# A hybrid decoder trunk on one core: the SSD branch product by seven half-size products, and gate multiplications on GpSimd

## Chip, core and metric

The kernel runs on one core of a Trainium2 chip. The metric is the time of one execution on the device, in microseconds (us). TensorE is called PE, its weight loads PEld, VectorE DVE, ScalarE ACT, GpSimd POOL; SP is the engine whose queue issues the DMA transfers.

## The reference

One layer of a decoder trunk with 1024 tokens and width 1024. The input is normalised and projected; three token mixers run side by side on the projection: attention in a window (branch A), gated linear attention, GLA (B), and a Mamba-2 state-space scan, SSD (C). Each mixer gives 512 channels, which a SiLU gate multiplies; each is projected to 1024 channels by its own matrix; sigmoid gates of the layer's input merge the three; an output projection and a residual add follow.

```python
y_a = sliding_window_attention(q, k, v, attn_sinks) * jax.nn.silu(ag)
y_b = rms_norm(o_b, gla_out_norm).reshape(b, s, GLA_VALUE_WIDTH) * jax.nn.silu(gg)
y_c = gated_group_rms_norm(y_c.reshape(b, s, SSD_D_INNER), sz, ssd_out_norm, SSD_GROUPS)
branches = jnp.stack([y_a, y_b, y_c], axis=2)
u = jnp.einsum("bsnw,nwd->bsnd", branches, w_branch)
gates = jax.nn.sigmoid(mg.reshape(b, s, N_BRANCH, D_MODEL))
merged = jnp.sum(gates * u, axis=2)
return x + merged @ w_out
```

## The kernel before

Activations lie with channels on partitions: a block of 128 channels by 512 tokens is one tile, and 1024 tokens are two halves. Every product keeps float32 precision by three matmuls: an operand is split into a rounded part (hi, an ACT cast to a 32-bit matmul format) and the remainder (lo, a subtraction), and hi·hi, hi·lo and lo·hi are added up in one PSUM bank.

Large projections by pairs of 128 output channels (`dense_pair`, called by `pair_fm`) use a seven-product form: the operand h is there in seven blocks or sums of blocks (11, 21, 22, t1, t2, t3, t4n), and seven products p1 to p7 take the place of eight. Weight sums and some remainders are made on POOL (lines 332 and 265). Such a pair is gg, which gives the gates of branch B: `branch_gates` (line 1050) takes its rows, loads the mixer's output (tile ggy, line 1056), forms the SiLU by a tanh on ACT and a multiplication on DVE (line 1058), multiplies (line 1059) and stores (line 1060) to ybg_d. It is called twice, for channels 0 and 2.

Then come the branch products. `load_y` loads a branch's 512 gated channels in eight blocks through three buffers (tags t1, t2, tx of the pool sums), casts each on ACT (line 1078) and makes its remainder on DVE (line 1079). `gated(n, d, y)` computes output block d (a unit) of branch n: it loads 128x512 weights, casts them on ACT, makes the remainder on DVE or POOL (line 265), loads the merge gate tg, and for each half runs 12 matmuls (line 1104) and one DVE multiplication by the gate (line 1107). The loop over d runs branch C (n = 2, tiles u2 in the order of instructions) two units ahead of branch A (n = 0); the sum of both goes to t_d (lines 1119, 1120). Then `merged` does branch B (n = 1), adds t_d, and `part` and `diff` make the seven sums for the output products (`dense_pair` on w_o).

The order of the instructions on each engine is set by a scheduler when the program is built: each engine, and SP's queue of transfers, then takes its own in that order and waits at the first that isn't ready. Buffers come from pools: big (14 tiles, held by h's seven sums until gg is done), big2 (4), sums (3), w2 (10 tiles of 128x512 for weights, sums and ggy), st (4 of 128x1024: gates and products), and PSUM in two pools of 4 banks.

Of the kernel before, what the change touches and what calls it, by code (L numbers as in the profile page):

```python
# [81 lines left out]
def kernel(  # L82
# [173 lines left out]
    def work(dt, name):  # L256
        return wpool.tile([P, 512], dt, tag="w2", bufs=NW2, name=name)
# [243 lines left out]
    for k in range(4):  # L501
# [10 lines left out]
                    in1=rowv[:, R_IF : R_IF + 32].unsqueeze(1).to_broadcast([P, NT, 32]), op=ALU.mult)  # L512
# [7 lines left out]
    first = True  # L520
    for a, i in ((a2, 3), (a1, 4), (a2, 2), (a1, 3), (a2, 1), (a1, 2), (a2, 0), (a1, 1), (a1, 0)):
# [8 lines left out]
        first = False  # L530
# [66 lines left out]
    with tc.tile_pool(name="att", bufs=2) as mp, tc.tile_pool(name="att1", bufs=1) as mp1:  # L597
# [63 lines left out]
        for t in range(NT):  # L661
            nk = P if t == 0 else 2 * P
            mk = amask[:, P * (1 - t % 2) : P * (1 - t % 2) + nk]
            nm = mp.tile([P, 8], F32, tag="nm", name=f"nm{t}")
# [34 lines left out]
            for g in range(2):  # L699
# [448 lines left out]
    for k in range(4):  # L1148
        b11, b12 = merged(k)
# [67 lines left out]
```

## Time and profile before

| | us |
|---|---|
| median of 3 runs (lowest, highest) | 998.47 (997.79, 998.58) |
| the profiled execution, its own time | 995.85 |
| its span, first to last instruction | 994.1 |
| PE busy in it | 944.2 |
| DVE busy | 765.0 |
| POOL busy | 491.2 |
| ACT busy | 451.1 |

Busy time of a group is the number of its instructions by their mean. A matmul's own duration (about 390 ns) overlaps with the next one's; what one adds to a row of them is the distance of their starts. "Idle before" is the time an engine stood still ahead of an instruction, with what ended it. Times in a timeline or a window count from the span's start.

### The profile page before, as it was taken

To read this page: it belongs to the slowest core of one execution; us is meant where nothing else is said; L and a number is where in the kernel's file an instruction comes from. 1 tells how busy PE (TensorE), PEld (TensorE's weight loads), DVE (VectorE), ACT (ScalarE), POOL (GpSimd) and SP (SyncE) were. 2 spreads that over 40 slices of the span, in tenths; PEclk is the share of its full clock that TensorE was granted. 3 is DMA by queue.
4 is the path that set the end of the run, shared out by engine and by line. 5 is a ranking of instruction groups with operands and counts; after the bars stand their busy time and mean duration, and the time that the engine had idled before them with its cause. 6 is when DMAs were issued, how large, how long until landed. Compare 5 with 4: busy or idle time off the path is not lost.

```text
span 994.1 us, 14844 instructions
## 1 busy us (share of the span) xinstructions
PE 944.2 (95%) x5089; PEld 795.8 (80%) x5089; DVE 765.0 (77%) x1228; ACT 451.1 (45%) x1014; POOL 491.2 (49%) x442
## 2 busy tenths in 40 slices
PE   8989888999999998999989999999999999997998
PEld 7989788988868777778778887878887878875786
DVE  6899787877998988876887858667868754599644
ACT  6442344366566556556545555344444411133221
POOL 5754556854562662344455644454533001256776
PEclk9999889999999999999999999999999999999999
DMA  9402142423232332241595635365465876763443
GB/s 365 180 27 85 54 160 67 142 88 111 78 119 85 107 97 99 77 136 42 193 297 190 210 129 157 120 201 180 128 209 199 280 239 217 239 207 103 163 146 116
DMA packets 84410, 150.14 MB, mean 151 GB/s; under 512 B 7328, under 2 KB 40304, under 8 KB 84336
## 3 DMA queue, kind: packets, MB, share of 16 engines
q1 hardware_dynamic: 84160, 149.18, 45.0%
q8 instruction: 40, 0.66, 0.3%
q14 instruction: 34, 0.28, 0.1%
q10 hardware_dynamic: 176, 0.02, 0.0%
HBM read 101.96 MB, written 47.22 MB: 150 GB/s over the span
## 4 chain that ended last, share of the span: by engine, by line
PE 40%; DVE 12%; DMA 8%; issue 7%; POOL 5%; ACT 5%; SPq 0%; POOLq 0%; DVEq 0%; ACTq 0%
PE ps_p_mg L320 14%; PE ps_p_o L320 5%; PE ps_p_ag L320 4%; PE ps_u L1104 3%; PE ps_p_cv L320 3%; DMA tg<-tg_d 2%; PE ps_p_gqk L320 2%; DVE acc L749 1%; DMA tl<-t_d 1%; DMA yc_r<-yc_d 1%; PE py L928 1%; PE ppv L715 1%; DMA yb_r<-ybg_d 1%; POOL s_o L332 1%; PE psc L677 1%
## 5 line engine op out<-in xcount | busy, mean ns | idle before, releaser
L320 PE MATMUL ps_p_mg<-ht_hi,wh_p_mg 128*128 128x512 f32 x192 | 75.9, 395 | 0.0
L320 PE MATMUL ps_p_mg<-ht_lo,wh_p_mg 128*128 128x512 f32 x192 | 75.7, 394 | 0.0
L320 PE MATMUL ps_p_mg<-ht_hi,wl_p_mg 128*128 128x512 f32 x192 | 75.7, 395 | 0.0
L340 DVE TENSOR_TENSOR c_mg<-ps_p_mg,c_mg 128x512 f32<-128x512 f32 x84 | 56.3, 681 | 12.6 <-PE ps_p_mg L320 8.1
L265 POOL TENSOR_TENSOR wl_p_mg<-s_mg,wh_p_mg 128x512 fp32r<-128x512 f32 x24 | 33.7, 1404 | 54.0 <-ACT wh_p_mg L262 46.3
L265 POOL TENSOR_TENSOR wl_u<-wr_u,wh_u 128x512 fp32r<-128x512 f32 x8 | 10.6, 1331 | 98.6 <-ACT wh_u L262 98.5
L320 PE MATMUL ps_p_mg<-h_hi,wl_p_mg 128*128 128x512 f32 x144 | 57.1, 396 | 0.0
L320 PE MATMUL ps_p_mg<-h_lo,wh_p_mg 128*128 128x512 f32 x144 | 56.6, 393 | 0.0
L320 PE MATMUL ps_p_mg<-h_hi,wh_p_mg 128*128 128x512 f32 x144 | 56.5, 392 | 0.0
L1107 DVE SCALAR_TENSOR_TENSOR tg<-tg,ps_u 128x512 f32<-128x512 f32 x48 | 31.9, 682 | 27.1 <-DMA tg<-tg_d 26.2
L262 ACT CAST wh_p_mg<-s_mg 128x512 fp32r<-128x512 f32 x48 | 29.6, 617 | 49.0 <-POOL s_mg L332 31.0
L265 DVE TENSOR_TENSOR wl_p_mg<-wr_mg,wh_p_mg 128x512 fp32r<-128x512 f32 x36 | 38.4, 1074 | 15.7 <-ACT wh_p_mg L262 8.9
L749 DVE SCALAR_TENSOR_TENSOR acc<-c_cv,cwh,acc 128x512 f32<-128x512 f32 (+3 forms) x48 | 41.8, 888 | 4.7 <-ACT acc L746 4.6
L320 PEld LDWEIGHTS ps_p_mg<-ht_hi,wh_p_mg 128*128 128x128 f32 x192 | 36.1, 188 | 7.2
L320 PEld LDWEIGHTS ps_p_mg<-ht_hi,wl_p_mg 128*128 128x128 f32 x192 | 36.1, 188 | 7.2
L320 PEld LDWEIGHTS ps_p_mg<-ht_lo,wh_p_mg 128*128 128x128 f32 x192 | 36.1, 188 | 7.1
L342 DVE SCALAR_TENSOR_TENSOR c_o<-ps_p_o,c_o 128x512 f32<-128x512 f32 x28 | 18.9, 688 | 26.5 <-POOL c_o L346 16.7
L690 ACT ACTIVATE sc<-sc,nm 128x256 f32<-128x256 f32 (+1 forms) x64 | 30.9, 485 | 18.1 <-DVE nm L685 18.1
L262 ACT CAST wh_u<-wr_u 128x512 fp32r<-128x512 f32 x24 | 14.7, 620 | 47.1 <-PE ps_u L1104 43.8
L733 ACT ACTIVATE c_mg<-c_mg 128x1024 f32<-128x1024 f32 x24 | 25.4, 1056 | 15.3 <-DVE c_mg L340 12.5
L320 PEld LDWEIGHTS ps_p_mg<-h_lo,wh_p_mg 128*128 128x128 f32 x144 | 27.1, 188 | 5.4
L320 PEld LDWEIGHTS ps_p_mg<-h_hi,wl_p_mg 128*128 128x128 f32 x144 | 27.1, 188 | 5.3
(479 smaller groups left out, 3456.8 us busy)
## 6 DMA issues: line engine op xcount, KB each, us to landing
wr_mg<-in_w_fm_dram SPq DMA_DIRECT2D x24, 512.0 KB, 4.0
tg_d<-c_mg SPq DMA_DIRECT2D x24, 512.0 KB, 2.6
tg<-tg_d SPq DMA_DIRECT2D x24, 512.0 KB, 4.3
wr_u<-in_w_br_dram SPq DMA_DIRECT2D x24, 256.0 KB, 3.9
xq<-in_xf_dram SPq DMA_DIRECT2D x8, 512.0 KB, 10.7
wr_cv<-in_w_fm_dram SPq DMA_DIRECT2D x8, 512.0 KB, 3.5
xbc_d<-acc SPq DMA_DIRECT2D x16, 256.0 KB, 2.6
e<-acs_dram SPq DMA_DIRECT2D x16, 256.0 KB, 5.4
```

The costliest lines, as they stand in the source:

```text
L262: A.copy(hi[:, :n], raw)
L265: (lo_eng or V).tensor_tensor(out=lo[:, :n], in0=raw, in1=hi[:, :n].bitcast(F32), op=ALU.subtract)
L320: T.matmul(ps, lhsT=l[:, k, :], rhs=r, start=n == 0, stop=n == 3 * kt - 1)
L332: G.tensor_tensor(out=o, in0=a, in1=b, op=op)
L340: V.tensor_tensor(out=o, in0=p, in1=c, op=op)
L342: V.scalar_tensor_tensor(out=o, in0=p, scalar=scale, in1=c, op0=ALU.mult, op1=op)
L677: T.matmul(psc[:, 256 * j : 256 * j + nk], lhsT=qT[:, h, :], rhs=kT[:, g, l, :nk], start=l == 0, stop=l == 1)
L690: A.activation(out=sc[:, j, :nk], in_=sc[:, j, :nk], func=AF.Exp, bias=nm[:, h : h + 1], accum_out=dn[:, h : h + 1])
L733: A.activation(out=c, in_=c, func=AF.Tanh, scale=0.5)
L749: V.scalar_tensor_tensor(out=acc[:, z:], in0=r[:, o + z - d : o + 512 - d], scalar=cwh[:, 4 * c + 3 - d : 4 * c + 4 - d], in1=acc[:, z:], ...
L1104: T.matmul(ps, lhsT=l[:, k, :], rhs=r, start=m_ == 0, stop=m_ == 11)
L1107: V.scalar_tensor_tensor(out=o, in0=o, scalar=1.0, in1=ps, op0=ALU.add, op1=ALU.mult)
```

## The change

`branch_gates` takes the engine for its last multiplication as an argument; for gg it is POOL, for branch A's gates it stays DVE. Branch C's operand is no longer four blocks per half but seven: 11, 21, 22 are blocks of its 2 x 2 division (channels by tokens), t3, t1, t2, t4n differences made on POOL; each has two parts k of 128x512 and is split by ACT and DVE as before. The blocks and t3 are made around the first gg pair (`y_blocks`), the other sums after the second (`y_sums`), for which the raw blocks are loaded again. `gated_pair` computes two units at once from weight blocks and sums of 128x256 by seven products of six matmuls, with the sums of weights on POOL, and the combinations of products on DVE and ACT in the tile cr. Remainders of the weights are made on POOL, but for the first two products. Branch A's weight remainders move from DVE to POOL too, and the loop goes by pairs.

```diff
-    def branch_gates(u0, f, y, dst, name):
+    def branch_gates(u0, f, y, dst, name, eng=V):
...
-                V.tensor_tensor(out=ys, in0=ch, in1=ys, op=ALU.mult)
+                eng.tensor_tensor(out=ys, in0=ch, in1=ys, op=ALU.mult)
...
-    y_c = load_y(big2_tile, yc_d, "yc", lambda: branch_gates(U_GG, 0, yb_d, ybg_d, "gg"))
-    branch_gates(U_GG, 2, yb_d, ybg_d, "gg")
+    def y_raw(f, hf, tag):
+        raw = sums.tile([P, 512], F32, tag=tag, name=f"yc_r{f}{hf}")
+        Q.dma_start(raw, yc_d[:, f, hf * 512 : hf * 512 + 512])
+        return raw
...
+    def y_part(key, k, a):
...
+        hi, lo = (p[:, k, :] for p in y_c[key])
+        A.copy(hi, a)
+        V.tensor_tensor(out=lo, in0=a, in1=hi.bitcast(F32), op=ALU.subtract)
+
+    def y_diff(key, k, o, a, b):
+        G.tensor_tensor(out=o, in0=a, in1=b, op=ALU.subtract)
+        y_part(key, k, o)
+
+    def y_blocks(k):
+        b12, b22 = y_raw(k, 1, "t2"), y_raw(k + 2, 1, "tx")
+        y_part("11", k, y_raw(k, 0, "t1"))
+        y_part("22", k, b22)
+        y_diff("t3", k, b12, b22, b12)
+        y_part("21", k, y_raw(k + 2, 0, "t1"))
+
+    def y_sums(k):
+        b11, b12, b22 = y_raw(k, 0, "t1"), y_raw(k, 1, "t2"), y_raw(k + 2, 1, "tx")
+        y_diff("t1", k, b11, b12, b11)
+        b21 = y_raw(k + 2, 0, "t2")
+        y_diff("t2", k, b22, b22, b11)
+        y_diff("t4n", k, b21, b21, b22)
+
+    y_blocks(0)
+    branch_gates(U_GG, 0, yb_d, ybg_d, "gg", G)
+    y_blocks(1)
+    branch_gates(U_GG, 2, yb_d, ybg_d, "gg", G)
+    for k in range(2):
+        y_sums(k)
...
+    def gated_pair(n, d):
+
+        raw = wpool.tile([P, 1024], F32, tag="wraw", name=f"wr_u{n}_{d}")
...
+        cr = big_tile(F32, f"cr{n}_{d}")
+        c11, c12, c21, c22 = (cr[:, i, :] for i in range(4))
+
+        def mul(w, key, ps, nm, first=True, last=True, eng=G):
+            wt = work(F32R, f"wp_u{n}_{d}{nm}")
+            A.copy(wt[:, :256], w)
+            eng.tensor_tensor(out=wt[:, 256:], in0=w, in1=wt[:, :256].bitcast(F32), op=ALU.subtract)
+            m_ = 0
+            for k in range(2):
...
+                for l, r in ((hi, r_hi), (hi, r_lo), (lo, r_hi)):
+                    T.matmul(ps, lhsT=l, rhs=r, start=first and m_ == 0, stop=last and m_ == 5, skip_group_check=True)
...
+        b1 = mtile(f"ps_u{n}_{d}_p1")
+        G.tensor_tensor(out=s1, in0=a21, in1=a22, op=ALU.add)
+        mul(a11, "11", b1, "p1", last=False, eng=V)
+        A.copy(c11, b1)
+        b2 = bank("p2")
+        mul(a12, "21", b2, "p2", eng=V)
+        G.tensor_tensor(out=a21, in0=a11, in1=a21, op=ALU.subtract)
+        G.tensor_tensor(out=s2, in0=s1, in1=a11, op=ALU.subtract)
+        V.tensor_tensor(out=c11, in0=b2, in1=c11, op=ALU.add)
+        gate(c11, 0, 0)
+        b7 = bank("p7")
+        mul(a21, "t3", b7, "p7")
+        mul(s2, "t2", b1, "p6", first=False, last=False)
+        A.copy(c12, b1)
+        G.tensor_tensor(out=a12, in0=a12, in1=s2, op=ALU.subtract)
+        V.tensor_tensor(out=c22, in0=b7, in1=c12, op=ALU.add)
+        b5 = bank("p5")
+        mul(s1, "t1", b5, "p5")
...
+        mul(a22, "t4n", b4, "p4")
...
+        mul(a12, "22", b1, "p3", first=False)
...
-    for d in range(KT + 2):
+    for d in range(0, KT + 2, 2):
...
-            tcs[d] = gated(2, d, y_c)
+            crs[d] = gated_pair(2, d)
...
-            tc_, ta = tcs.pop(d - 2), gated(0, d - 2, y_a)
...
+                ta = gated(0, d - 2 + i, y_a, G)
```

How the order moves, at three places. First, POOL after the last gg product's weight remainder (wl_p3_gg2; s and wl are weight sums and remainders). Before:

```order
L332 TENSOR_TENSOR s3_gg2_7943<-wr_gg2_1_7879,wr_gg2_2_7881 128x512
L265 TENSOR_TENSOR wl_p5_gg2_7982<-s1_gg2_7903,wh_p5_gg2_7981 128x512
L332 TENSOR_TENSOR s4_gg2_8000<-wr_gg2_1_7879,s2_gg2_7923 128x512
L265 TENSOR_TENSOR wl_p3_gg2_8003<-s4_gg2_8000,wh_p3_gg2_8002 128x512
L265 TENSOR_TENSOR wl_u1_0_8730<-wr_u1_0_8727,wh_u1_0_8729 128x512
```

Now (yc_r are raw blocks of branch C, numbered by channel block and half, and the sums made in their place; ggy the gate multiplications of branch B; s_u2, wr_u2 and wp_u2 weight sums and remainders of the first pair):

```order
L265 TENSOR_TENSOR wl_p3_gg2_8005<-s4_gg2_8002,wh_p3_gg2_8004 128x512
L1108 TENSOR_TENSOR yc_r20_8060<-yc_r20_8060,yc_r21_8054 128x512
L1186 TENSOR_TENSOR s_u2_0_8091<-wr_u2_0_8088 128x256
L1191 TENSOR_TENSOR wr_u2_0_8088<-wr_u2_0_8088 128x256
L1192 TENSOR_TENSOR s_u2_0_8091<-s_u2_0_8091,wr_u2_0_8088 128x256
L1059 TENSOR_TENSOR ggy200_8023<-c1_gg2_7885,ggy200_8023 128x512
L1169 TENSOR_TENSOR wp_u2_0p7_8124<-wr_u2_0_8088,wp_u2_0p7_8124 128x256
L1199 TENSOR_TENSOR wr_u2_0_8088<-wr_u2_0_8088,s_u2_0_8091 128x256
L1169 TENSOR_TENSOR wp_u2_0p6_8133<-s_u2_0_8091,wp_u2_0p6_8133 128x256
L1169 TENSOR_TENSOR wp_u2_0p5_8146<-s_u2_0_8091,wp_u2_0p5_8146 128x256
L1059 TENSOR_TENSOR ggy20512_8030<-c1_gg2_7885,ggy20512_8030 128x512
L1108 TENSOR_TENSOR yc_r10_8070<-yc_r11_8072,yc_r10_8070 128x512
```

Where POOL had nothing until branch B's weights, 20 instructions follow up to the second t4n sum: the eleven below the first row here, then one remainder, a gate multiplication, a weight sum of the second pair, a remainder, the last gate multiplication, the second t2 sum, two weight sums, and the second t4n sum.

Second, PE after the last gg product, in branch C's first two pairs (ps_u2_0 and ps_u2_2; p1 holds p1, p6 and p3 one after the other; the operand's name tells which). Before, 12 matmuls of one unit and half follow 12 of the next. Now, from the 27th matmul of branch C on:

```order
L1175 MATMUL ps_u2_2_p1_8227<-yc11_7680,wp_u2_2p1_8229 128x512 x2
L1175 MATMUL ps_u2_2_p2_8239<-yc21_7692,wp_u2_2p2_8240 128x512 x2
L1175 MATMUL ps_u2_2_p1_8227<-yc11_7680,wp_u2_2p1_8229 128x512 x4
L1175 MATMUL ps_u2_2_p2_8239<-yc21_7692,wp_u2_2p2_8240 128x512 x4
L1175 MATMUL ps_u2_0_p5_8145<-yct1_8057,wp_u2_0p5_8146 128x512
L1175 MATMUL ps_u2_0_p4_8157<-yct4n_8067,wp_u2_0p4_8158 128x512
L1175 MATMUL ps_u2_0_p5_8145<-yct1_8057,wp_u2_0p5_8146 128x512 x2
L1175 MATMUL ps_u2_0_p1_8097<-yct2_8063,wp_u2_0p6_8133 128x512
L1175 MATMUL ps_u2_2_p7_8253<-yct3_7687,wp_u2_2p7_8254 128x512 x2
L1175 MATMUL ps_u2_0_p1_8097<-yct2_8063,wp_u2_0p6_8133 128x512 x2
L1175 MATMUL ps_u2_0_p4_8157<-yct4n_8067,wp_u2_0p4_8158 128x512
L1175 MATMUL ps_u2_2_p7_8253<-yct3_7687,wp_u2_2p7_8254 128x512 x4
```

The second pair's first two products have moved in between the first pair's k = 0 and k = 1 parts; the row yct4n in the last but one place is the 48th matmul of branch C and the first that reads the second t4n block.

Third, SP's queue, from the loads of the second `y_sums` on. Before, six of the eight loads of branch A's operand (ya_r) were issued among the gg transfers. Now:

```order
L1096 DMA yc_r10_8070<-yc_d_4740 128x512
L1096 DMA yc_r31_8074<-yc_d_4740 128x512
L1096 DMA yc_r11_8072<-yc_d_4740 128x512
L1060 DMA ybg_d_2918<-ggy200_8023 128x512
L1060 DMA ybg_d_2918<-ggy20512_8030 128x512
L1161 DMA tg2_2_8222<-tg_d_2916 128x1024
L1096 DMA yc_r30_8079<-yc_d_4740 128x512
L1060 DMA ybg_d_2918<-ggy210_8037 128x512
L171 DMA wr_u0_1_8350<-in_w_br_dram 128x512
L1060 DMA ybg_d_2918<-ggy21512_8044 128x512
L1161 DMA tg2_3_8224<-tg_d_2916 128x1024
L1076 DMA ya_r00_8186<-yag_d_2917 128x512
```

All loads of branch A's operand have moved behind the last loads of branch C's and behind the stores of branch B's last gate multiplications.

## Rows read from the trace of the kernel before

**Rows 1.** Page: busy time and share of each engine; the span in 40 slices.
```profile
PE 944.2 (95%) x5089; PEld 795.8 (80%) x5089; DVE 765.0 (77%) x1228; ACT 451.1 (45%) x1014; POOL 491.2 (49%) x442
...
PEclk9999889999999999999999999999999999999999
```

**Rows 2.** Windows: busy PE, PEld, DVE, ACT, POOL; clock, DMA share, GB/s.
```profile
768.00:857.00 89.00, 87.38 (x385) 71.73 (x384) 50.85 (x73) 20.05 (x34) 5.14 (x4) 1.00 0.72 241
904.00:936.00 32.00, 26.67 (x103) 19.52 (x102) 27.11 (x30) 11.14 (x19) 25.12 (x18) 0.95 0.34 116
...
726.00:857.00 131.00, 127.25 (x559) 103.78 (x558) 84.26 (x117) 39.34 (x68) 19.96 (x14) 1.00 0.70 233
```

**Rows 3.** Chain that ended last, in order of time: start us, us, what.
```profile
813.71 32.94 PE ps_u L1104 x144
```

**Rows 4.** Timeline of PE: start us, us, line, operation, out<-in.
```profile
768.11 0.39 PE L1104 MATMUL ps_u<-yc_hi,wh_u 128*128 128x512 f32 x1
...
769.92 0.39 PE L1104 MATMUL ps_u<-yc_hi,wl_u 128*128 128x512 f32 x1
...
857.34 0.39 PE L1104 MATMUL ps_u<-yb_hi,wh_u 128*128 128x512 f32 x1
```

**Rows 5.** Waits of PE, 740 to 860: total us, times, longest.
```profile
PE ps_p_gg L320 <- ACT wh_p_gg L262: 1.9, 2, 1.1
PE ps_u L1104 <- DVE tg L1107: 1.6, 2, 1.2
```

**Rows 6.** Groups of DVE from 726 to 768: busy us, mean ns, idle before.
```profile
L340 DVE TENSOR_TENSOR c_gg<-ps_p_gg,c_gg 128x512 f32<-128x512 f32 x13 | 8.7, 683 | 1.7 <-PE ps_p_gg L320 1.6
L1079 DVE TENSOR_TENSOR yc_lo<-yc_r,yc_hi 128x512 fp32r<-128x512 f32 x8 | 7.0, 909 | 2.6 <-ACT yc_hi L1078 2.6
L265 DVE TENSOR_TENSOR wl_p_gg<-wr_gg,wh_p_gg 128x512 fp32r<-128x512 f32 x4 | 4.1, 1018 | 1.7 <-ACT wh_p_gg L262 1.7
```

**Rows 7.** Groups of the whole span by form: DVE and ACT.
```profile
L1107 DVE SCALAR_TENSOR_TENSOR tg<-tg,ps_u 128x512 f32<-128x512 f32 x48 | 31.9, 682 | 27.1 <-DMA tg<-tg_d 26.2 <-PE ps_u L1104 0.8
L645 DVE TENSOR_TENSOR qh<-qk,qh 128x256 fp32r<-128x256 f32 x24 | 13.5, 577 | 0.8 <-ACT qh L644 0.7
L644 ACT CAST qh<-qk 128x256 fp32r<-128x256 f32 x24 | 8.9, 404 | 16.1 <-DVE qk L632 16.0
```

**Rows 8.** A group of ACT from 726 to 768.
```profile
L1078 ACT CAST yc_hi<-yc_r 128x512 fp32r<-128x512 f32 x8 | 4.9, 620 | 8.6 <-DMA yc_r<-yc_d 8.6
```

**Rows 9.** Groups of POOL by form.
```profile
L629 POOL TENSOR_TENSOR t<-qk,tb 128x256 f32<-128x256 f32 x16 | 12.8, 820 | 8.5 <-issue 2.8 <-ACT c_cv L752 1.8 <-ACT es L687 1.7
L265 POOL TENSOR_TENSOR wl_p_gg<-s_gg,wh_p_gg 128x512 fp32r<-128x512 f32 x4 | 5.9, 1470 | 15.9 <-ACT wh_p_gg L262 8.4 <-DVE ggy L1059 7.5
```

**Rows 10.** Timeline of POOL: start us, us, what, idle before.
```profile
759.79 1.74 POOL L332 TENSOR_TENSOR s_gg<-wr_gg,s_gg 128x512 f32<-128x512 f32 x1
762.26 1.57 POOL L265 TENSOR_TENSOR wl_p_gg<-s_gg,wh_p_gg 128x512 fp32r<-128x512 f32 x1 [0.73 <-ACT wh_p_gg L262]
836.31 1.29 POOL L265 TENSOR_TENSOR wl_u<-wr_u,wh_u 128x512 fp32r<-128x512 f32 x1 [72.48 <-ACT wh_u L262]
```

**Rows 11.** Line 629's instructions: ns min/median/max, two forms together.
```profile
L629 POOL TENSOR_TENSOR t<-qk,tb x32: 315/740/1193, 156.9 to 369.5; 128x256 f32<-128x256 f32 x16, 128x64 f32<-128x64 f32 x16
```

**Rows 12.** Timeline of DVE behind the last gg product.
```profile
773.18 0.68 DVE L1059 TENSOR_TENSOR ggy<-c_gg,ggy 128x512 f32<-128x512 f32 x1
```

**Rows 13.** Timeline of SP's queue: issues of the operands' loads.
```profile
733.28 1.58 SPq L1076 DMA_DIRECT2D yc_r<-yc_d  x3
...
764.99 1.76 SPq L1076 DMA_DIRECT2D ya_r<-yag_d  x2
```

**Rows 14.** Loads of yc_r, then of ya_r: us from issue to landing.
```profile
DMA to landing us min/median/max: 3.0/4.1/5.2
...
DMA to landing us min/median/max: 2.8/5.5/7.1
```

**Rows 15.** DMA issues from 715 to 800: count, KB each, median us to landing.
```profile
tg<-tg_d SPq DMA_DIRECT2D x6, 512.0 KB, 5.7
```

More of the change, by code (lines that the diff above doesn't have):

```diff
@@ L1088 @@
     merge_gates(1, U_MGB, 6)
-    y_c = load_y(big2_tile, yc_d, "yc", lambda: branch_gates(U_GG, 0, yb_d, ybg_d, "gg"))
-    branch_gates(U_GG, 2, yb_d, ybg_d, "gg")
+    y_c = {}
+    def y_raw(f, hf, tag):
[3 more added lines that the diff above has]
+    def y_part(key, k, a):
+        if k == 0:
+            t = (big_tile if key in ("t1", "t2", "t4n") else big2_tile)(F32R, f"yc{key}")
+            y_c[key] = (t[:, 0:2], t[:, 2:4])
+        hi, lo = (p[:, k, :] for p in y_c[key])
[22 more added lines that the diff above has]
+        y_sums(k)
     def gated(n, d, y, lo_eng=None):
@@ L1108, in gated, with bank, gate @@
         return tg
+    def gated_pair(n, d):
+        raw = wpool.tile([P, 1024], F32, tag="wraw", name=f"wr_u{n}_{d}")
+        for i in range(2):
+            Q.dma_start(raw[:, 512 * i : 512 * i + 512], w_br[8 * n + d + i])
+        a11, a12, a21, a22 = (raw[:, 256 * i : 256 * i + 256] for i in range(4))
+        s = work(F32, f"s_u{n}_{d}")
+        s1, s2 = s[:, :256], s[:, 256:]
+        tgs = []
+        for i in range(2):
+            tg = st_tile(f"tg{n}_{d + i}")
+            Q.dma_start(tg, tg_d[n, d + i])
+            tgs.append(tg)
+        cr = big_tile(F32, f"cr{n}_{d}")
[6 more added lines that the diff above has]
+            for k in range(2):
+                r_hi, r_lo = (p[:, k, :] for p in y_c[key])
+                hi, lo = wt[:, k * P : k * P + P], wt[:, 256 + k * P : 256 + k * P + P]
+                for l, r in ((hi, r_hi), (hi, r_lo), (lo, r_hi)):
+                    T.matmul(ps, lhsT=l, rhs=r, start=first and m_ == 0, stop=last and m_ == 5, skip_group_check=True)
+                    m_ += 1
+        def bank(nm):
+            return psd1.tile([P, 512], F32, tag="d1", name=f"ps_u{n}_{d}_{nm}")
+        def gate(c, i, hf):
+            V.scalar_tensor_tensor(out=c, in0=tgs[i][:, hf * 512 : hf * 512 + 512], scalar=1.0, in1=c, op0=ALU.add, op1=ALU.mult)
+        b1 = mtile(f"ps_u{n}_{d}_p1")
[16 more added lines that the diff above has]
+        mul(s1, "t1", b5, "p5")
+        e5 = half_tile(f"p5_u{n}_{d}")
+        A.copy(e5, b5)
+        b4 = bank("p4")
+        mul(a22, "t4n", b4, "p4")
+        V.tensor_tensor(out=c21, in0=b4, in1=c22, op=ALU.add)
+        gate(c21, 1, 0)
+        V.tensor_tensor(out=c22, in0=e5, in1=c22, op=ALU.add)
+        gate(c22, 1, 1)
+        mul(a12, "22", b1, "p3", first=False)
+        V.tensor_tensor(out=c12, in0=b1, in1=e5, op=ALU.add)
+        gate(c12, 0, 1)
+        return cr
@@ L1110 @@
     t_d = dram.tile([KT, P, S], F32, name="t_d")
-    tcs = {}
-    for d in range(KT + 2):
+    crs = {}
+    for d in range(0, KT + 2, 2):
         if d == 2:
@@ L1115 @@
         if d < KT:
-            tcs[d] = gated(2, d, y_c)
+            crs[d] = gated_pair(2, d)
         if d >= 2:
-            tc_, ta = tcs.pop(d - 2), gated(0, d - 2, y_a)
-            V.tensor_tensor(out=tc_, in0=tc_, in1=ta, op=ALU.add)
-            Q.dma_start(t_d[d - 2], tc_)
+            cr = crs.pop(d - 2)
+            for i in range(2):
+                ta = gated(0, d - 2 + i, y_a, G)
+                V.tensor_tensor(out=ta, in0=ta, in1=cr[:, 2 * i : 2 * i + 2, :].rearrange("p f l -> p (f l)"), op=ALU.add)
+                Q.dma_start(t_d[d - 2 + i], ta)
     y_b = load_y(big_tile, ybg_d, "yb")
```

## The prediction

> **What bounds the kernel now.** I read the page first: TensorE is busy 95% of the span, DVE 77%, the other two under half, and TensorE's granted clock is at its upper level, 2.4 GHz, in nearly every slice [rows 1]. Then the stages around the change [rows 2]: from 768 to 857 us, where the SSD and attention branch products run, PE has 87.4 of 89 us, DVE 50.9, ACT 20.1, POOL 5.1. So PE bounds this stage. Between 904 and 936 it has holes: 26.7 of 32. The chain of waits goes straight through the branch products: 32.94 us of nothing but matmuls [rows 3]. The timeline of PE gives the frame [rows 4]: the first SSD product starts at 768.11 (I call this moment E), the first GLA product at 857.34, so 89.2 us for 384 matmuls; eight steps from 768.11 to 769.92 are 1.81 us, 0.227 us per matmul, 87.1 us in all. Some 2.1 us of the stage is idle, 1.6 of them behind a gate multiplication of DVE; the product before E loses 1.9 us to ACT casts [rows 5].
>
> What reaches the end: a later start of the GLA products moves everything behind them, since their tail is bound by DVE work that starts with them. I take 1:1.
>
> **The change, part by part.**
>
> *Matmuls.* A pair of units has 48 matmuls now, 7 products x 2 blocks x 3 = 42 afterwards; four pairs: 24 fewer, all of the same 128x512 form. 24 x 0.227 = **-5.4 us**.
>
> *Work of DVE and ACT.* DVE loses 8 gate multiplications and 16 weight remainders of 0.68 us (-16.3), gains 20 sums of 0.68, 8 half-width remainders of 0.58 and 6 operand remainders of 0.91 (+23.7) [rows 6, 7]: +7.4 us on a DVE with 38 us free from 768 to 857 [rows 2]. ACT gains about 28 half casts at 0.40 against 8 at 0.62, 12 copies and 6 casts at 0.62: +17 on 20 of 89 us [rows 2, 7, 8]. As sums both are hidden by the free time of these engines; in order, they are not, which the DVE rival below prices.
>
> *Work of POOL.* Added: 8 gate multiplications and 8 operand sums at 1.47, 36 half-width ones at 0.82, 8 weight remainders of the attention units at 1.29: 23.5 + 29.5 + 10.3 = 63 us, on 20 busy of the 131 us from 726 to 857 [rows 2, 9, 10]. As a sum that fits too, and POOL now stands still for 72.48 us there [rows 10]. What matters is the order. In the queue of POOL after the remainder for the last gg product, 20 instructions stand up to and with the second t4n sum, which the first pair needs: 8 of 512 columns (3 operand sums k=1, one k=0, 4 gate multiplications) and 12 of 256. None may be passed.
>
> Wide price: 1.47 mean, with ends 1.29 and 1.74 [rows 9, 10]. Narrow price: 128x256 is measured elsewhere at 0.82 mean, which I take; the low end is a straight line from the shortest 64-column one (0.315) to 1.29 at 512 columns, 0.73; the high end for a mean of twelve is half of 1.74, 0.87 (one alone took up to 1.19) [rows 9 to 11]. Chain: 8 x 1.47 + 12 x 0.82 = 21.6 us (19.1 to 24.4), and an ACT cast of 0.6. In the same time PE has only 10 matmuls of the last gg product and 47 in front of the first that reads the second t4n block: 57 x 0.227 = 12.9 us. If POOL gets to the queue's head when PE does, PE stands still for 21.6 + 0.6 - 12.9 = **+9.3 us** (6.8 to 12.1).
>
> A head start lowers that. Now the last gg remainder ends at 763.83 [rows 10], 2.0 us before PE wants it (E minus 10 matmuls = 765.84). But it has a floor, because the gate multiplications need the last gg product itself: the second now starts 5.1 us after E [rows 12], no sooner than 3 us (DVE add, tanh, DVE gate, 0.7 each, and issue). From that one on, 6 wide and 5 narrow remain: 11.4 us at the low prices, so the block is there at E + 15.0, and PE asks for it at E + 47 x 0.227 = 10.7. So the stall is at least 4.3 us unless a price is lower than any row.
>
> The Trainium skill's page "SBUF — State Buffer", section "Who interferes with whom", says that a DVE instruction with two SBUF inputs and a GpSimd instruction that reads SBUF exclude each other for their whole length, which speaks against moving multiplications from one to the other. The trace agrees so far: DVE adds with one operand in PSUM keep to 0.683, remainders with both in SBUF have means of 0.909 and 1.018 in the stretch with POOL work [rows 6]. By that rule as a strict one, each POOL step would stand behind DVE's, at the high end of the chain (24.4), and the time would be 1009.7; by the mean rows it is the sum below.
>
> *Operand of SSD.* Instead of 8 loads through three buffers there are 16, and six of them pass one buffer (t1), one after the other: r00, r20, r10, r30, then r00 again for the first sum. A link is load 4.1, cast 0.62, remainder 0.91: 5.6 us [rows 6, 8, 14]. The first lands near 738.4 (third of three issues from 733.28 on, 0.5 apart) [rows 13], its remainder is done at 739.9; three links give 756.7, the reload lands at 760.8. Behind it on POOL, in order: sum t1, two instructions of gg, sum t2, and the last gg remainder, 5 x 1.47: 768.2. Ten matmuls later E is 770.4 instead of 768.1. At the shortest loads (3.0) a link is 4.3 and nothing shifts. Range 0 to 2.4, taken: **+2 us**, since the median load is nearer.
>
> *Operand of the attention branch.* Its loads use the same three buffers, so they now start after the t1, t2, t4n sums of k=1, where today six of eight are issued before 768 [rows 13]. Through t1 go r00, r03, r10 (links of 5.5 + 0.62 + 0.68 = 6.8 us) [rows 6, 8, 14]. The third hi part is there 3 x 6.8 - 0.7 = 19.7 us after the second t2 sum; PE asks for it 3.1 us (one wide and two narrow POOL steps to the t4n sum) + 0.6 (cast) + 49 x 0.227 = 14.8 us after that sum. Stall 4.9 us at the median load; none at the shortest (2.8). Taken: **+2.5 us**, the middle, since the median comes from a stretch with more transfers at a time.
>
> *The rest.* Eight loads more, 2 MB, raise the DMA share of 726 to 857 from 0.70 (233 GB/s, 30 MB) to about 0.75: hidden. A PE that waits can lose clock: between 904 and 936, with 26.7 of 32 us busy, it was granted 0.95 [rows 2]; 5% of the 26 us behind E is 1.3 us, an upper end that I leave out of the sum. Order and number of the GLA and output products stay.
>
> **Sum.** -5.4 + 2 + 9.3 + 2.5 = +8.4 us. The profiled execution took 995.85 us (span 994.1 and 1.75 around it), so it would be 1004.3; the median of the runs shown, 998.47, is 2.6 above the profiled one, and on it the sum gives **1006.9 us**. A difference under 0.2% (2 us) can't be told from none by such measurements.
>
> **Rivals.**
>
> *POOL hides everything, faster.* For it: POOL has 111 of 131 us free, and the first four products of a pair need only early blocks. Then -5.4 stands alone: 993.1, or 991 if the idle 2.1 goes too. It is decided at one place: the second t4n sum must end within 10 us of E. Against it: the gate multiplications in front of it wait for the last gg product, and the floor above gives 4.3. With the floor and no other stall, -1.1: 997.4. I give faster by over 2 us 0.18.
>
> *No change.* The stall lies between 3.4 and 7.4 in sum: floor case, or short loads with an early POOL; also if the tail's DVE work, not its start, sets the end. 998.5, chance 0.12.
>
> *DVE's queue stands at a gate load, much slower.* The first attention gate's load needs a buffer that the first pair's last gate frees, and behind its multiplication on DVE stand the second pair's sums, which hold PSUM banks that PE wants. A gate load takes 5.7 us [rows 15] and could come wholly on top: +14, 1012.6. For it: DVE already waits 26.2 us for gate loads today [rows 7]. Against: PE lost only 1.6 us to that [rows 5]. Chance 0.12.
>
> The forecast itself, slower by 2 to 12 us, has 0.58. So faster 0.18, same 0.12, slower 0.70. The range goes from 995.3 (floor -1.1 and the idle 2.1 recovered) to 1016 (12.1 + 2.4 + 4.9 - 5.4 = +14.0, and 3.5 of a gate load or of lost clock).
>
> **What would show it.** Right: PE has 24 fewer matmuls; between E and the first attention product PE idles 7 to 12 us, put down to ACT casts and POOL; POOL is over 80% busy for 25 us from E; the t4n sum of k=1 ends 16 to 20 us after E; E is at 768 to 771; the GLA products start 6 to 12 us later than 857.3. Each stage's matmuls keep 0.227 us. Wrong: half-width POOL work far under 0.73, the second t4n sum within 10 us of E, or GLA products starting before 857.

## The result, and the profile after

The changed kernel takes 1011.79 us (median of 4 runs, 1010.65 to 1013.16), the kernel before, on the same chip, 998.13 us (4 runs, 994.81 to 998.58). The ratio is 1.0135, 95% interval 1.0111 to 1.016: slower by 13.7 us. The prediction said 1006.9, between 995.3 and 1016.0.

The page of the changed kernel, busy time and clock by slices; before, in [rows 1], DVE had 765.0, POOL 491.2, and the clock was below the top digit in two slices instead of four:

```profile
PE 952.8 (94%) x5065; PEld 797.4 (79%) x5065; DVE 785.5 (78%) x1238; ACT 466.6 (46%) x1052; POOL 558.7 (55%) x502
...
PEclk9999988999999999999999999999999899998999
```

TensorE has 24 matmuls fewer (5065 against 5089) and is busy 8.6 us longer. The timeline of PE in the changed kernel gives the stages by four starts: the first gg product, the first SSD product (E), the first attention product, the first GLA product.

```profile
727.74 0.39 PE L320 MATMUL ps_p_gg<-h_hi,wh_p_gg 128*128 128x512 f32 x1
...
774.31 1.98 PE L1175 MATMUL ps_u_p<-yc,wp_u_0p 128*128 128x512 f32 x8
...
782.79 2.42 PE L1175 MATMUL ps_u_p<-yc,wp_u_2p 128*128 128x512 f32 x8 [0.25 <-ACT wp_u_2p L1168]
...
786.96 0.63 PE L1175 MATMUL ps_u_p<-yct,wp_u_0p 128*128 128x512 f32 x2
792.19 0.80 PE L1175 MATMUL ps_u_p<-yct,wp_u_0p 128*128 128x512 f32 x1 [4.60 <-ACT yct L1104]
...
804.04 0.50 PE L1144 MATMUL ps_u<-ya_hi,wh_u 128*128 128x512 f32 x1 [1.10 <-ACT p_u L1204]
...
872.42 0.39 PE L1144 MATMUL ps_u<-yb_hi,wh_u 128*128 128x512 f32 x1
```

Windows over the same four stages (columns as in [rows 2]), the kernel before:

```profile
726.54:768.11 41.57, 39.45 (x173) 31.70 (x172) 32.95 (x44) 19.11 (x33) 14.82 (x10) 1.00 0.65 217
768.11:784.43 16.32, 16.32 (x73) 13.52 (x72) 13.45 (x22) 6.97 (x12) 0.00 (x0) 1.00 0.96 340
784.43:857.34 72.91, 71.29 (x313) 58.41 (x312) 37.66 (x51) 13.11 (x23) 5.14 (x4) 1.00 0.67 218
857.34:994.10 136.76, 124.08 (x529) 99.22 (x527) 93.85 (x112) 38.12 (x64) 87.45 (x60) 0.99 0.48 160
```

and the changed kernel, where the last two rows cut out the wait of 4.60 us and what follows it:

```profile
727.74:774.31 46.57, 41.50 (x173) 32.47 (x172) 32.47 (x37) 18.91 (x33) 28.45 (x20) 0.96 0.67 217
774.31:804.04 29.73, 21.97 (x74) 14.45 (x72) 20.02 (x23) 14.16 (x31) 29.11 (x27) 0.89 0.63 196
804.04:872.42 68.38, 66.04 (x288) 54.01 (x289) 58.16 (x70) 21.47 (x43) 32.45 (x28) 1.00 0.74 244
872.42:1011.50 139.08, 126.71 (x529) 101.19 (x527) 92.81 (x110) 38.23 (x64) 86.07 (x60) 0.96 0.48 157
...
787.40:792.10 4.70, 0.19 (x1) 0.00 (x0) 0.00 (x0) 1.17 (x2) 4.70 (x6) 1.00 0.64 209
792.10:798.00 5.90, 5.30 (x12) 3.54 (x13) 4.01 (x4) 4.35 (x11) 5.90 (x7) 0.50 0.67 190
```

The two profiled spans differ by 17.4 us and the medians by 13.7: the profiled execution of the changed kernel lies 1.4 over its median, that of the kernel before 2.3 under. The 17.4 lie so: 1.2 ahead of gg, 5.0 in the gg stage, 13.4 between E and the first attention product, -4.5 up to the GLA products, 2.3 in the tail. The first is not the change's: that start lies anywhere from 723.2 to 729.5 in the profiles below. In the second window PE is busy 21.97 us for the 72 matmuls that took 16.32, and idle for 7.8: it waits, and then runs at the lower clock. Behind the 4.60 us the granted clock is 0.50, the level of 1.2 GHz, and 12 matmuls take 6.2 us (792.19 to 798.40, 0.5 of it a second wait) instead of 2.7.

POOL's timeline in the changed kernel shows what those 4.60 us waited for: the cast of the second t2 sum, which POOL makes from 790.22 on. The first row is the last gg remainder, the last the second t4n sum:

```profile
770.53 1.29 POOL L265 TENSOR_TENSOR wl_p_gg<-s_gg,wh_p_gg 128x512 fp32r<-128x512 f32 x1
771.78 1.74 POOL L1108 TENSOR_TENSOR yc_r<-yc_r,yc_r 128x512 f32<-128x512 f32 x1
...
790.22 1.26 POOL L1108 TENSOR_TENSOR yc_r<-yc_r,yc_r 128x512 f32<-128x512 f32 x1
791.44 0.72 POOL L1191 TENSOR_TENSOR wr_u<-wr_u 128x256 f32<-128x256 f32 x1
792.12 0.73 POOL L1192 TENSOR_TENSOR s_u<-s_u,wr_u 128x256 f32<-128x256 f32 x1
792.81 1.72 POOL L1108 TENSOR_TENSOR yc_r<-yc_r,yc_r 128x512 f32<-128x512 f32 x1
```

Twenty instructions without a gap of note, 771.8 to 794.5: 22.7 us.

### The profile page after: what moved, and what is told of

The parts are those of the page before. It is cut to its first block, busy times and chain, and to the rows that moved or that the text cites. A ratio compares the mean times of both kernels' runs of the same rounds, so it can differ in the third digit from the quotient of the medians.

```text
span 1011.5 us, 14965 instructions
## 1 busy us (share of the span) xinstructions
PE 952.8 (94%) x5065; PEld 797.4 (79%) x5065; DVE 785.5 (78%) x1238; ACT 466.6 (46%) x1052; POOL 558.7 (55%) x502
## 4 chain that ended last, share of the span: by engine, by line
PE 42%; DVE 15%; issue 8%; POOL 7%; DMA 7%; ACT 5%; SPq 0%; POOLq 0%; DVEq 0%; ACTq 0%
PE ps_p_mg L320 12%; PE ps_p_o L320 5%; PE ps_u L1144 4%; PE ps_p_ag L320 4%; PE ps_p_gv L403 3%; PE ps_p_cv L320 2%; DVE acc L749 2%; PE ps_p_gqk L320 2%; PE ps_u_p L1175 2%; DMA tl<-t_d 1%; DVE sc L680 1%; DVE c_mg L340 1%; DVE wl_p_mg L265 1%; ACT sc L690 1%; PE psc L677 1%
## 5 line engine op out<-in xcount | busy, mean ns | idle before, releaser
L749 DVE SCALAR_TENSOR_TENSOR acc<-c_cv,cwh,acc 128x512 f32<-128x512 f32 (+3 forms) x48 | 41.9, 889 | 4.9 <-ACT acc L746 4.8
L265 POOL TENSOR_TENSOR wl_u<-wr_u,wh_u 128x512 fp32r<-128x512 f32 x16 | 23.8, 1497 | 38.5 <-ACT wh_u L262 24.3
L320 PEld LDWEIGHTS ps_p_mg<-ht_hi,wl_p_mg 128*128 128x128 f32 x192 | 36.2, 189 | 7.8 <-DVE wl_p_mg L265 0.7
L320 PEld LDWEIGHTS ps_p_mg<-ht_lo,wh_p_mg 128*128 128x128 f32 x192 | 36.2, 189 | 7.1
L342 DVE SCALAR_TENSOR_TENSOR c_o<-ps_p_o,c_o 128x512 f32<-128x512 f32 x28 | 18.9, 688 | 27.5 <-POOL c_o L346 17.4
L320 PEld LDWEIGHTS ps_p_mg<-h_hi,wh_p_mg 128*128 128x128 f32 x144 | 27.2, 189 | 5.4
L1144 PE MATMUL ps_u<-yb_hi,wh_u 128*128 128x512 f32 x64 | 25.9, 405 | 3.0 <-DVE tg L1147 3.0
```

Of the source, the lines that this page charges most:

```text
L265: (lo_eng or V).tensor_tensor(out=lo[:, :n], in0=raw, in1=hi[:, :n].bitcast(F32), op=ALU.subtract)
L320: T.matmul(ps, lhsT=l[:, k, :], rhs=r, start=n == 0, stop=n == 3 * kt - 1)
L342: V.scalar_tensor_tensor(out=o, in0=p, scalar=scale, in1=c, op0=ALU.mult, op1=op)
L749: V.scalar_tensor_tensor(out=acc[:, z:], in0=r[:, o + z - d : o + 512 - d], scalar=cwh[:, 4 * c + 3 - d : 4 * c + 4 - d], in1=acc[:, z:], ...
```

## The experiments

Twelve kernels, each timed beside the kernel before (medians of 997.3 for e1 to e4, 997.7 for e5 to e8, 997.9 for e9 to e11, 998.3 for e12). The profiled execution of each is cut at the same four starts (us; "head" is E to the first attention product, "rest" from there to the first GLA product, "branch" both):

| | time (ratio, 95% interval) | gg | head | rest | branch | tail |
|---|---|---|---|---|---|---|
| before | | 41.6 | 16.3 | 72.9 | 89.2 | 136.8 |
| the change | 1011.8 (1.0111 to 1.016) | 46.6 | 29.7 | 68.4 | 98.1 | 139.1 |
| e1 gates on DVE | 1011.3 (1.012 to 1.0194) | 43.1 | 27.3 | 69.9 | 97.2 | 143.2 |
| e2 gates alone | 1004.0 (1.0058 to 1.0091) | 44.9 | 16.3 | 75.7 | 92.0 | 136.5 |
| e3 shorter t1 chain | 1014.3 (1.0145 to 1.0204) | 46.1 | 32.7 | 66.1 | 98.8 | 145.3 |
| e4 sums on DVE | 1015.5 (1.0161 to 1.0203) | 45.7 | 26.8 | 73.3 | 100.1 | 140.3 |
| e5 gates left out | 1009.0 (1.0083 to 1.0138) | 40.9 | 31.6 | 66.2 | 97.7 | 141.0 |
| e6 ten remainders left out | 1004.9 (1.0056 to 1.0099) | 46.1 | 26.0 | 67.0 | 93.0 | 138.7 |
| e7 pairs' POOL work left out | 1005.4 (1.0046 to 1.01) | 40.4 | 27.0 | 66.7 | 93.8 | 138.8 |
| e8 first pair of eight products | 1015.2 (1.0154 to 1.0224) | 40.3 | 36.2 | 72.5 | 108.6 | 139.2 |
| e9 e7, k=1 blocks in w2 | 1002.1 (1.0017 to 1.0057) | 44.9 | 21.6 | 65.0 | 86.6 | 140.0 |
| e10 e1, k=1 blocks in w2 | 1007.7 (1.0067 to 1.0127) | 45.1 | 28.9 | 64.1 | 92.9 | 142.5 |
| e11 e1, all blocks in w2 | 1013.8 (1.012 to 1.0193) | 54.9 | 23.7 | 63.9 | 87.7 | 143.6 |
| e12 e8, k=1 blocks in w2 | 1012.1 (1.0115 to 1.0182) | 41.9 | 30.1 | 72.1 | 102.2 | 138.3 |

A stage comes from one execution each, and these lie between 3.7 us under the kernel's median (e7) and 3.8 over it (e3); so the stages tell where the time is, and the ratios how much it is. Two more cautions: each edit also changes the order that the scheduler gives to the other instructions, so the head holds 72 matmuls in some kernels and up to 82 in others (e8); and the branch stage counts from E, so where the gg stage shrinks, part of a wait for the operand can move from gg into branch.

**e1.** Theory: POOL's queue alone makes the second t2 and t4n sums late. Rival: DVE does.

```diff
-    branch_gates(U_GG, 0, yb_d, ybg_d, "gg", G)
+    branch_gates(U_GG, 0, yb_d, ybg_d, "gg")
```

and the same for channel 2.

> The change, with the eight GLA gate multiplications back on DVE. Theory (POOL's queue makes the k=1 operand sums late): four wide POOL steps fall out in front of the second t2 and t4n sums, some 6 us. The wait of 4.6 us ahead of the second t2 block shrinks to 0 to 2 us, TensorE keeps the upper clock level behind it, and the GLA products start 5 to 10 us sooner than 872.4. Time about 1003 (1001 to 1007). E stays near 774, because the chain of loads through buffer t1 is the same. Rival (DVE is what is late; its queue or its share of SBUF): DVE gets 8 x 0.68 us more in the same place, so 1012 or slower. [...]

Four wide instructions left POOL's queue, and the branch stage lost 0.9 us. The scheduler put weight sums and remainders of the second pair in their place: the second t4n sum ends 19.9 us after E (20.2 before), with POOL busy 24.1 of the 27.3 us of the head. DVE, with 23.7, is now waited for as well (PE stands 2.3 us for a weight remainder). Neither theory came out: POOL and DVE are both nearly full. Only the gg stage recovered, 3.4 us (E came at 766.4, not near 774), and the tail of this execution is 4.1 longer: the medians differ by 0.5.

**e2.** The kernel before with `branch_gates(..., G)` for gg, and nothing else.

> The kernel before, with only the GLA gate multiplications moved to POOL. Theory: POOL has nothing else after the last gg product there, so only the gg stage can feel it, by buffers that come free later and by weight remainders queued behind gates: 0 to +3 us, 998 to 1001. Rival (a POOL multiplication beside DVE work costs DVE as much time as it takes, in a stage where DVE then holds PE): 8 x 1.5 = up to +12, 1005 or slower.

A miss, between the theory and the rival: 6.7 us by the medians, by the ratio's interval at least 5.8. The gg stage grew by 3.4, as much as e1 gave back. That it is the gates shows over all the kernels with three raw buffers: with gates on POOL the gg stage takes 44.9 to 46.6 (five kernels), with gates on DVE or left out 40.3 to 43.1 (five, the kernel before among them). The rest grew by 2.8; there PE waited 3.09 us for one of DVE's multiplications by a merge gate, where it had waited 1.6 for two. DVE lost the gate multiplications and yet was no less busy in the gg stage (33.4 us for 39 instructions, before 33.0 for 44), because what stayed took longer. Two groups of DVE there, e2:

```profile
L1079 DVE TENSOR_TENSOR yc_lo<-yc_r,yc_hi 128x512 fp32r<-128x512 f32 x8 | 9.9, 1262 | 4.7 <-ACT yc_hi L1078 4.7
L340 DVE TENSOR_TENSOR c_gg<-ps_p_gg,c_gg 128x512 f32<-128x512 f32 x13 | 8.7, 682 | 1.7 <-PE ps_p_gg L320 1.6
```

In [rows 6] the first took 909 ns, the second 683: the operation with both inputs in SBUF pays, the one that reads PSUM doesn't.

**e3.** Raw block 3 (first half) goes through tx, so that t1 has one link less ahead of its reload.

```diff
-        y_part("21", k, y_raw(k + 2, 0, "t1"))
+        y_part("21", k, y_raw(k + 2, 0, ("t1", "tx")[k]))
```

> The change, with one raw block (channel block 3, first half) loaded through buffer tx instead of t1, so that the chain of loads through t1 has three links before the reload and not four. Theory (the t1 chain sets E): the reload of block 0 starts about 6 us sooner (755 instead of 761.8), the last gg remainder on POOL ends 3 to 5 us sooner, E at 769 to 771 instead of 774.3, time 1007 to 1009. If E is set by casts and remainders queued in front of the gg weights on ACT and DVE instead, E stays within 1.5 us of 774 and the time at 1011 to 1012. The POOL stall behind E stays or grows by up to 2 us, since the gate multiplications still need the last gg product.

The reload started 4.5 us sooner (757.28 instead of 761.78), but the gg stage stayed: 46.1 against 46.6 (E came at 772.3, 2.1 us sooner, 1.6 of them ahead of gg). The time lies over both expectations. POOL had no gap from 753 to 772, with gates and sums at 1.7 us each in front of the last gg remainder. So the chain through t1 exists, and does not set E.

**e4.** The three k=1 sums on DVE.

```diff
-        G.tensor_tensor(out=o, in0=a, in1=b, op=ALU.subtract)
+        (V if k == 1 and key != "t3" else G).tensor_tensor(out=o, in0=a, in1=b, op=ALU.subtract)
```

> The change, with the three k=1 operand sums (t1, t2, t4n) on DVE instead of POOL; gates stay on POOL. Theory (POOL's queue): these sums are no longer behind weight sums and gates; the second t4n block is there 5 to 9 us sooner, the 4.6 us wait falls under 2 us, the clock stays up, time 1001 to 1006. Rival (DVE's queue or a gate load holds the branch stage): three more DVE instructions in front of the pair's combinations, no gain, 1011 to 1014.

The rival's number. The second t4n sum ends 4.0 us sooner after E (16.2) and no wait of PE in the head is over 1.7, as the theory had it, but the time didn't follow: the head shrank by 3.0, the rest grew by 4.9 (PE waits 4.3 us for a cast of the attention operand). In the head now both engines are full (window of the head, e4):

```profile
774.87:801.63 26.76, 20.96 (x74) 13.52 (x72) 25.95 (x27) 13.08 (x30) 26.37 (x24) 0.94 0.64 209
```

**e5.** The multiplication by the GLA gates is skipped.

> The change with the eight GLA gate multiplications left out altogether, on POOL and on DVE (branch B's operand goes through without its gate). Moving them from POOL to DVE left the stage from the first SSD to the first GLA product at 97.2 us (98.1 with them on POOL). Theory (DVE and POOL share something and their work together is too much for the first 30 us, so that it doesn't matter which of them has it): leaving four gates out of that stretch saves what they occupy, 4 x 1.3 to 1.7: stage 91 to 93.5 us; the gg stage stays at 43 to 44 as with gates on DVE; time 1000 to 1006. Rival (the wait is in the order, operand loads or gate loads, not in the amount of work): stage 96 to 98, time 1007 to 1011.

The gg stage fell to 40.9, below before's; the branch stage stayed at 97.7, the rival's number. Most of that is a matter of where the stage begins: E came 5.0 us sooner in the span, the second t4n sum only 1.3 sooner, so it ends 23.9 us after E. POOL stood still ahead of none of the k=1 sums; whether they would have waited for their raw blocks with less work ahead of them, this run can't show.

**e6.** In `mul`, for the first two pairs:

```diff
+            full = eng is V or d > 2
+            if full:
                 eng.tensor_tensor(out=wt[:, 256:], ...
+                lo = wt[:, 256 + k * P : 256 + k * P + P] if full else hi
```

> The change with ten half-width weight remainders of the first two SSD pairs left out on POOL (their matmuls take the rounded part in place of the remainder). Gates stay on POOL. Theory (joint work of POOL and DVE): 10 x 0.72 to 1.19, some 9 us, fall out of the stretch between the first SSD and the first attention product: that stretch goes from 29.7 to 20 to 23 us, the stage from 98.1 to 88 to 92; gg stage unchanged at 46 to 47; time 1003 to 1007. Rival (gates behind the last gg product, or loads, set the end): stage over 95, time 1009 or more.

5.1 us off the branch stage, where 6 to 10 were expected, and the head takes 26.0 where 20 to 23 were. The time, 1004.9, lies in the theory's range, the stages between it and the rival.

**e7.** As e5 and e6, for all pairs, and without the four weight sums of line 1186 and following.

> The change with all of the pair's work on POOL left out: GLA gates, weight sums (raw blocks take their place) and half-width remainders of all four pairs. Left on POOL: the operand sums and attention's remainders. Theory: the 24 saved matmuls then show: stage 82 to 86 us (360 x 0.227 = 81.7 and some gate waits), gg stage 43 to 44, time 990 to 997. Rival (DVE's sums behind a gate load, or the operand's loads through three buffers, hold the stage by themselves): stage 88 or more, time over 998.

The gg stage is 40.4 and POOL almost empty behind it (7.9 of 27.0 us in the head), and still the head takes 27.0. The waits of POOL in it name the rest (waited for, total us, times, longest; e7):

```profile
POOL yc_r L1109 <- DMA yc_r<-yc_d: 13.3, 3, 6.3
```

The raw blocks of the k=1 sums are loaded through the same three buffers, each only when a k=0 sum has let go.

**e8.** Gates on DVE, operand block 12 split too, and the first pair by `gated`.

> The change with gates on DVE and the first SSD pair by the eight products of before (operand block 12 split as well); the other three pairs by seven products. 18 matmuls are saved instead of 24 (-4.1 us). Theory (too much joint work in the first 30 us): the first pair then needs no operand sums and no weight sums, so POOL has 10.9 us more before its first product is asked for: stage 85 to 91 us (before 89.2, the change 98.1), gg stage 43 to 45, time 996 to 1003. Rival (any seven-product pair costs more DVE and POOL time than it saves on TensorE): stage over 93, time over 1005.

A clear miss, 108.6, on the rival's side. POOL stood idle 7.0 us behind its first operand sums, and the k=1 sums ran from 29 to 35 us after E: their raw blocks were issued only from 784 to 796 us, E being 764.9.

**e9.** e7, and in `y_sums`, for k=1, raw blocks in `work` tiles (pool w2) instead of t1, t2, tx.

```diff
+        t1_, t2_, tx_, t3_ = ("w2",) * 4 if k in (1,) else ("t1", "t2", "tx", "t2")
-        b11, b12, b22 = y_raw(k, 0, "t1"), y_raw(k, 1, "t2"), y_raw(k + 2, 1, "tx")
+        b11, b12, b22 = y_raw(k, 0, t1_), y_raw(k, 1, t2_), y_raw(k + 2, 1, tx_)
```

> The run with the pair's POOL work left out (GLA gates, weight sums, half-width remainders), and the four raw blocks of the k=1 operand sums now in buffers of the w2 pool instead of the three of the sums pool. In that run POOL stood still three times for raw blocks (4.8, 6.4 and 2.2 us) and the stage from the first SSD to the first GLA product took 93.8 us. Theory (with POOL's queue gone, the reloads of the raw blocks through three buffers are the next bound): the loads are issued ahead, these waits go, the first attention product comes 17 to 20 us after the first SSD product instead of 27.0, the stage takes 84 to 88 us, time 992 to 999. Rival (DVE's queue or the lowered clock holds it): stage 92 or more, time as before, 1003 to 1006.

Branch stage 86.6, as the theory had it (the head a little longer than its 17 to 20); the median, 1002.1, is 3 us over, since the gg stage went back to 44.9 (PE waits 1.96 us ahead of E for a cast of the first weights). POOL's waits for raw blocks, then the window of the head, where the clock stays at 1.00, e9:

```profile
POOL yc_r L1109 <- DMA yc_r<-yc_d: 5.8, 2, 4.9
```

```profile
774.46:796.08 21.62, 18.94 (x74) 13.03 (x75) 18.03 (x27) 15.41 (x35) 8.39 (x6) 1.00 0.88 304
```

**e10.** The same buffers with nothing left out, on e1.

> The change with GLA gates on DVE (stage 97.2 us, 1011), and the four raw blocks of the k=1 sums in buffers of the w2 pool. Nothing is left out. Theory (two bounds of about the same length, POOL's queue and the reloads): POOL's 20 instructions up to the second t4n sum stay, some 20 us, so only what POOL waited for loads goes: stage 93 to 97, time 1005 to 1011. If the reloads alone were the bound: stage 85 to 90, time under 1002.

The number is as expected, the branch stage falls from 97.2 to 92.9, but the mechanism is not. The 20 instructions did not stay ahead of the second t4n sum: with its raw blocks there, the scheduler moved the three k=1 sums up, behind three of POOL's instructions, and the last ends 7.4 us after E. So the operand no longer holds the head, and the head still takes 28.9 us. Another limit now shows, DVE with 28.4 of them (PE waits 2.95 us for one of its weight remainders):

```profile
771.85:800.72 28.87, 21.94 (x78) 15.85 (x79) 28.37 (x31) 15.01 (x33) 25.67 (x23) 0.82 0.64 211
```

With e5, e7 and e9 this is nearly a square (no gates on POOL in all of it, but on DVE in two and left out in two): POOL's work out (97.7 to 93.8), reloads freed (97.2 to 92.9), both (86.6). By the branch stage each alone gives 4 us and both together 11; with the gg stage counted in, 4.4, 2.3, and 7.1 to 8.8 together; by the medians 3.7, 3.6, and 6.9 to 9.2. So both cost time, and e9 shows that the two together make up the loss of the branch stage. That they run side by side, so that one alone hides the other, is not shown: their sum is near what both give.

**e11.** As e10, for k=0 too.

> As the kernel with the k=1 raw blocks in the w2 pool and gates on DVE, but the raw blocks of k=0 in the w2 pool too, so that no operand sum waits for one of the three buffers and three loads of the attention operand go ahead. Theory: the gg stage ends sooner (41 to 43 us) unless its weights now wait for w2 buffers (then 44 to 47); stage behind it 91 to 96; time 1002 to 1009. If it falls under 998 the change pays with nothing but buffers.

A miss by the time. In front of E PE waits 11.90 us for the cast of the first weights, and ACT before it for remainders of the operand that read those raw blocks: the blocks hold the w2 buffers that the weights need (54.9 us of gg). Behind E the stage is short, 87.7.

**e12.** e8 with e10's buffers.

> Both bounds eased with nothing left out: gates on DVE, the first SSD pair by eight products (which gives POOL 10.9 us), and the four raw blocks of the k=1 sums in buffers of the w2 pool. With the first pair by eight products but three raw buffers the stage took 108.6 us, with POOL free between its sums. Theory (there the reloads alone held the sums): with loads ahead the stage falls to 86 to 93 us, time 997 to 1005. Rival (the later pairs' own work on POOL and DVE, or w2 buffers, hold it): stage over 97, time over 1008. Under 995.8 it would beat the kernel before; 18 fewer matmuls would allow 4.1 us at most.

A miss, on the rival's side: 102.2. PE waits 3.9 us for a cast of the third pair's weights and 3.2 for an ACT copy out of PSUM. Why these come late wasn't tried. No version beat the kernel before.

## Why the prediction was right, and which terms were not

The direction and the range held; the predicted time is 4.9 us under the measured one, and the sum was right in part by terms that cancel.

- *Matmuls, -5.4.* Right. 288 instead of 312 matmuls lie between the first attention and the first GLA product, and that part is 4.5 us shorter, with 0.7 more of waits in it.
- *POOL's queue, +9.3.* The chain is there as written: 22.7 us for the 20 instructions (21.6 said), the second t4n sum 20.2 us after E (16 to 20 said), PE idle 7.8 us (7 to 12 said), POOL busy 98% of the head. Wide ones took 1.55 on average in it (1.47 said), the twelve narrow ones 11.0 us, 0.92 each, over the upper end of 0.87. Of the 7.8 us, 4.60 lie ahead of the second t2 block, where the sum looked at t4n only, and 0.52 ahead of t4n. What failed is the reading that this queue alone would set the stall: reloads were priced ahead of E and for the attention operand, not for the k=1 blocks, whose sums still ended 18.6 us after E with the pairs' work off POOL (e7). Taking four gates off POOL (e1) changed 0.9 us of the branch stage.
- *DVE, +7.4, hidden.* Mis-sized: DVE's busy time rose by 20.5 us, from 765.0 to 785.5, for just the ten instructions more that were said. Most prices were those of an instruction alone. With the gates and the pairs' work off POOL (e7), DVE's same 1238 instructions take 773.9, near the forecast; the other 11.6 us are what DVE pays beside that work. In the branch stage DVE is busy 78.2 us now, 51.1 before.
- *E, +2.* Measured +5.0 in the gg stage, and by another mechanism (E at 774.3, 768 to 771 said). The step "six of them pass one buffer (t1)" described a real chain, whose reload came at 761.78 (756.7 said), but e3 shows that it doesn't decide. (At the shortest loads its link is 4.5 us by its own prices, not 4.3; nothing shifts by either.) 3.4 us belong to the gates (e2 against before, and the change against e1). The other 1.6 (e1 against before) stay open: with the same operand e5, e7 and e8 have a gg stage shorter than the kernel before. The failing step is the one that costed the gate multiplications only behind E: in the gg stage they were taken as hidden by POOL's free time, and they lengthen DVE's work there.
- *Attention operand, +2.5.* Not seen. In front of attention's products PE waited for a copy (1.10) and a sum (1.79) of the second SSD pair. It does appear where others go (4.3 in e4, 2.3 in e7).
- *Lost clock, left out, at most 1.3.* The largest error. The same matmuls keep PE busy 2.05 us longer in the gg stage, 5.6 in the head, 2.6 in the tail, some 10 of the 17.4 us between the profiles. Not all of it is the clock (0.96, 0.89 and 0.96 in these stages): in the head the 12 matmuls at 0.50 cost 3.0 us more. Most of the other 2.6 are slower starts around waits at a clock of 1.00, as in the eight matmuls from 782.79 on, 2.42 us, against 1.98 for the eight from 774.31.
- *One to one to the end.* The GLA products start 15.1 us later (6 to 12 said), the span ends 17.4 later; the other 2.3 are the tail. Tails of the twelve run from 136.5 to 145.3, with up to 10.2 us of waits at GLA's gate multiplications (e3). The two kernels without seven-product pairs have the shortest (before 136.8, e2 136.5), all others 138.3 or more; why wasn't tried.
- *The rivals.* "POOL hides everything" was decided where the text said, at the second t4n sum: 20.2 us after E, not 10. The gate-load rival's time, 1012.6, is near the result by chance: PE waited 0.6 and 1.8 us for the sums of which it spoke.
- *The rule on two SBUF inputs.* The strict reading, 1009.7, was nearer than the mean rows, though its chain, 24.4 us, was not reached (22.7) and the lost clock was not in it: the nearness is partly luck. The two timelines of the changed kernel show it, POOL first, then DVE:

```profile
742.89 1.29 POOL L1059 TENSOR_TENSOR ggy<-c_gg,ggy 128x512 f32<-128x512 f32 x1 [0.93 <-DMA ggy<-yb_d]
...
756.17 1.65 POOL L1059 TENSOR_TENSOR ggy<-c_gg,ggy 128x512 f32<-128x512 f32 x1 [3.13 <-DVE c_gg L1058]
757.79 1.72 POOL L332 TENSOR_TENSOR s_gg<-wr_gg,wr_gg 128x512 f32<-128x512 f32 x1
759.47 3.44 POOL L1059 TENSOR_TENSOR ggy<-c_gg,ggy 128x512 f32<-128x512 f32 x2
```

```profile
756.61 1.76 DVE L265 TENSOR_TENSOR wl_p_gg<-s_gg,wh_p_gg 128x512 fp32r<-128x512 f32 x1
758.30 1.76 DVE L1058 SCALAR_TENSOR_TENSOR c_gg<-ggt,c_gg 128x512 f32<-128x512 f32 x1
759.98 1.77 DVE L1105 TENSOR_TENSOR yc<-yc_r,yc 128x512 fp32r<-128x512 f32 x1
761.67 0.68 DVE L340 TENSOR_TENSOR c_gg<-ps_p_gg,c_gg 128x512 f32<-128x512 f32 x1
...
764.15 0.68 DVE L1058 SCALAR_TENSOR_TENSOR c_gg<-ggt,c_gg 128x512 f32<-128x512 f32 x1
```

Alone, POOL's multiplication takes 1.29 and DVE's line 1058 takes 0.68. Side by side, 756.17 to 762.91, four of POOL and three of DVE take 6.7 us, where 4 x 1.29 + 3 x 0.68 is 7.2: they take turns, and little runs at once. One turn is 1.7 us (756.61 to 758.30), 0.3 under the sum of the two alone. The addition that reads PSUM (761.67) keeps its 0.68 beside POOL. The Trainium skill, "SBUF — State Buffer", section "Who interferes with whom", says that two such instructions exclude each other and that a DVE instruction with one SBUF input goes free; by this trace the first holds but for those 0.3 us a turn, and the second holds. So a multiplication that moves from DVE to POOL takes up to 1.29 us of what both share, where it took up to 0.68. How much of the 3.4 us in the gg stage comes from that, and how much from buffers that the later gates free later, was not separated.

What stays open: the tail, 1.6 us of the gg stage, the branch stages of e8 and e12, and whether another order of the work could feed the pairs from these buffers.

## What to carry to other kernels

A fast product with fewer matmuls pays only if its extra sums and reloads are ready when TensorE gets there: sum up the queue of each engine and the chain of buffers up to the first product that needs the last operand, all of them, since another can become the bound when the longest goes. Don't count an engine's idle time as room for work whose inputs lie in SBUF while the other of DVE and POOL works on SBUF too. And price a wait of TensorE with the matmuls behind it, at the lower clock.

## What was not expected of the hardware

One stand of 4.7 us (0.19 us busy) was followed by some 6 us at a granted clock of 0.50, which cost another 3 us. And DVE and POOL very nearly take turns: 1.76 instead of 0.68 us on DVE, 1.72 instead of 1.29 on POOL, in the same 6.7 us.
